# Two row maxima of a wide tile joined into one, in a NaN-ignoring row maximum

## The chip, the cores and the metric

The kernel runs on one core of one Trainium2 chip. The core has engines that work side by side, each with its own instruction stream: VectorE (DVE in the profile), ScalarE (ACT), GpSimd (POOL), TensorE (PE, unused here) and SyncE (SP), which issues the DMA transfers. They wait for one another through semaphores. The 16 DMA engines move data between the device's main memory (HBM) and the on-chip memory, which has 128 partitions.

The metric is the time of one execution on the device, in microseconds (us). Lower is better.

## The reference

```python
batch, seq, dim = 32, 2048, 2048
x = np.random.randn(batch, seq, dim).astype(np.float32)
mask = np.random.rand(batch, seq, dim) < 0.1
x[mask] = np.nan
...
return np.nanmax(x, axis=-1).astype(np.float32)
```

The input has 65,536 rows of 2048 float32 numbers, 512 MiB, a tenth of them NaN. The output is the maximum of each row without the NaNs, 256 KiB. Every input byte is read once, and little is done with it.

## The kernel before

**Tiles and quarter rows.** Each partition gets 512 rows, and a quarter row (Q = 512 elements, 2 KiB in a partition) is the unit of all tables. `TILES` is a list of tiles; each says how it is loaded, how it is worked on, and how the maxima are taken. Tile 0 has 4 quarter rows. Tiles 1 to 32 are the wide ones: 32 quarter rows, that is 8 whole rows in each of 128 partitions, 8 MiB, loaded by one DMA. Tiles 33 to 68 are cut in other ways and mostly have 28 quarter rows.

**What is done to a tile.** Ahead of the maximum the upper 16 bits of every element are turned into a key and then written back, in place, such that a NaN becomes something small. The steps for a wide tile are:

- *Key* on ScalarE (ACT, the program's line 299): three passes over 12, 12 and 8 quarter rows, as each is free. They read the upper halves of `xt` (an access of every second 16-bit number) and write them back as unsigned keys. A pass waits only for the load of its tile.
- *Write* on GpSimd (POOL, L309): one multiply-add that turns keys into the number's upper half again. Of the first 12 quarter rows, 5 are written by VectorE (a TENSOR_SCALAR over 128x2560, which the profile shows under L316, the line of the helper) and 7 by POOL (128x3584). Then POOL writes 12 (128x6144) and 8 (128x4096). A write waits for its key pass.
- *Maximum* on VectorE (L316, TENSOR_REDUCE into `acc`): the last list of a tile says over how many quarter rows each step goes. `128x3` in a profile row is a step over 3 rows, that is 12 quarter rows; `128x2` is 8, `128x5` is 20. A step waits for the writes of the quarter rows it covers.

In one tile's entry `([12], [(5, -1), 7])` reads: a key pass of 12, then a write of 5 on VectorE (-1) and one of 7 on POOL.

**What sets the order.** Nothing reorders instructions: each engine runs its own in the order in which the loop over tiles writes them. For each key pass the loop issues the pass, then the writes whose keys are then complete, then the maxima (`maxima`) whose quarter rows have all been given a write. VectorE's stream in a wide tile is thus: its write of 5, and the maxima. The class `Order` adds the semaphore waits, leaving out those that another wait already covers.

**Buffers and loads.** There are three buffers (`BUFS = 3`), used in turn. The load of tile n goes into the buffer of tile n - 3 and waits for the last maximum of that tile:

```python
                if state["red"] == len(reds):
                    free[number % BUFS] = [state["end"]]
```

All loads are issued from SP's queue, one behind the other, by line 495 (the first one by L286). The results are stored at the end (L591), after some steps (L331, L345 on POOL, L323 on VectorE) that turn rows of nothing but NaN into NaN, one part of the rows at a time. POOL's steps for a part stand two to four tiles after the part's last tile (two for the wide ones).

Of the kernel before, what the change touches and what calls it, by code (L numbers as in the profile page):

```python
# [15 lines left out]

TILES = (
    [([4], [([4], [4])], [4])]
    + [([32], [([12], [(5, -1), 7]), ([12], [12]), ([8], [8])], [12, 12, 8])] * 32
# [622 lines left out]
```

## Time and profile before

| | us |
|---|---|
| median of 3 runs | 1252.22 (1252.11 to 1252.24) |
| the profiled execution | 1252.06 |
| its span in the profile | 1250.3 |
| VectorE busy | 1164.8 |
| ScalarE busy | 1151.3 |
| GpSimd busy | 1060.2 |

The span is the time between the first and the last recorded event; the execution's own time is 1.8 us longer. A row of the chain of waits or of the timeline begins with its start and its length in us, then the engine, the line, and what was written from what; "x2" means that two instructions stand in one row, and the brackets tell how long the engine was idle ahead of it and for whom. A row of the groups has, behind the bar, the busy time in us, the mean of one instruction in ns, and the idle time ahead of such instructions. In the list of DMA issues the last number is the median time from issue to landing in us.

### The profile page before, as it was taken

How to read it: one execution, taken by the hardware profiler on the slowest of the kernel's cores; microseconds unless marked ns; L12 is line 12 of the kernel's file. 1: busy time of each engine (PE TensorE's matmuls, PEld its weight loads, DVE VectorE, ACT ScalarE, POOL GpSimd, SP SyncE). 2: the span in 40 equal slices, each digit the busy share in tenths (PEclk: the TensorE clock that was granted, in tenths of full speed). 3: DMA queues.
4: the chain of work that ended last, by engine and by line, in shares of the span. 5: the costliest groups of instructions: out<-in, count | busy, mean ns of one | idle time of the engine just before them, and what ended most of it. 6: DMA issues, size and time to landing. Idle time of an engine off the chain costs nothing.

```text
span 1250.3 us, 1057 instructions
## 1 busy us (share of the span) xinstructions
DVE 1164.8 (93%) x252; ACT 1151.3 (92%) x294; POOL 1060.2 (85%) x253
## 2 busy tenths in 40 slices
DVE  0799999999999999999999998988889989999999
ACT  3999999999999999999999999898888789999998
POOL 0888788887988888888899998977999887999988
DMA  9999999999999999999999999999999999999997
GB/s 411 428 436 436 436 436 436 436 437 434 436 436 432 432 432 428 434 430 434 434 431 438 433 439 440 433 427 431 440 428 440 426 439 431 431 430 428 432 427 309
DMA packets 17240, 537.21 MB, mean 430 GB/s; under 512 B 2640, under 2 KB 2640, under 8 KB 5712
## 3 DMA queue, kind: packets, MB, share of 16 engines
q1 hardware_dynamic: 17232, 537.14, 99.5%
q14 instruction: 8, 0.07, 0.0%
HBM read 536.87 MB, written 0.26 MB: 430 GB/s over the span
## 4 chain that ended last, share of the span: by engine, by line
DMA 38%; DVE 25%; ACT 23%; POOL 14%; issue 1%; SPq 0%; ACTq 0%
DMA xt<-in_x_dram 38%; DVE acc L316 24%; ACT xt L299 21%; POOL xt L309 14%; ACT kt L299 2%; SPq L495 0%; SPq L286 0%; DVE acc L323 0%; SPq L637 0%; ACTq L183 0%; SPq L293 0%
## 5 line engine op out<-in xcount | busy, mean ns | idle before, releaser
L316 DVE TENSOR_REDUCE acc<-xt 128x3 f32<-128x6144 f32 (+3 forms) x219 | 1114.6, 5135 | 64.2 <-POOL xt L309 56.7
L309 POOL TENSOR_SCALAR xt<-xt 128x3584 int16<-128x3584 uint16 (+9 forms) x204 | 926.3, 4541 | 162.8 <-ACT xt L299 152.9
L299 ACT ACTIVATE xt<-xt 128x6144 uint16<-128x6144 int16 (+12 forms) x236 | 1006.3, 4361 | 62.8 <-DMA xt<-in_x_dram 61.9
L309 POOL TENSOR_SCALAR xt<-kt 128x4096 int16<-128x4096 uint16 (+10 forms) x34 | 128.8, 3789 | 21.2 <-ACT kt L299 19.7
L299 ACT ACTIVATE kt<-xt 128x4096 uint16<-128x4096 int16 (+10 forms) x42 | 118.9, 2852 | 29.7 <-DMA xt<-in_x_dram 29.4
L316 DVE TENSOR_SCALAR xt<-xt 128x2560 int16<-128x2560 uint16 x32 | 52.6, 1644 | 19.0 <-ACT xt L299 19.0
L299 ACT ACTIVATE xt<-kt 128x1536 int16<-128x1536 uint16 (+6 forms) x14 | 29.6, 2112 | 0.2
L331 POOL TENSOR_SCALAR late<-acc 128x112 int32<-128x112 f32 (+1 forms) x5 | 2.8, 558 | 0.4
L299 ACT ACT_TABLE_LOAD x1 | 1.3, 1283 | 1.3 <-SPq L293 1.3
L345 POOL TENSOR_TENSOR acc<-acc,late 128x112 int32<-128x112 int32 (+1 forms) x5 | 2.0, 397 | 0.4
L351 POOL MEMSET scalars<- 128x1 f32 x1 | 0.1, 98 | 0.9 <-SPq L293 0.9
L623 POOL MEMSET const-float32-0.0<- 128x1 f32 x1 | 0.1, 98 | 0.2 <-issue 0.2
L299 ACT ACTIVATE scalars<-scalars 128x1 f32<-128x1 f32 x1 | 0.2, 203 | 0.0
L323 DVE SCALAR_TENSOR_TENSOR acc<-acc 128x7 f32<-128x7 f32 x1 | 0.2, 166 | 0.0
L623 POOL MEMSET const-bfloat16-1.0<- 128x1 bf16 x1 | 0.1, 101 | 0.0
L623 POOL MEMSET const-uint8-127<- 128x1 uint8 x1 | 0.1, 101 | 0.0
L623 POOL MEMSET const-float32-1.0<- 128x1 f32 x1 | 0.1, 98 | 0.0
## 6 DMA issues: line engine op xcount, KB each, us to landing
xt<-in_x_dram SPq DMA_DIRECT2D x20, 7168.0 KB, 23.3
xt<-in_x_dram SPq DMA_DIRECT2D x5, 2304.0 KB, 25.6
xt<-in_x_dram SPq DMA_DIRECT2D x2, 5632.0 KB, 19.6
xt<-in_x_dram SPq DMA_DIRECT2D x3, 3584.0 KB, 25.0
xt<-in_x_dram SPq DMA_DIRECT2D x2, 4352.0 KB, 17.3
xt<-in_x_dram SPq DMA_DIRECT2D x2, 4096.0 KB, 19.7
xt<-in_x_dram SPq DMA_DIRECT2D x1, 7680.0 KB, 24.2
xt<-in_x_dram SPq DMA_DIRECT2D x9, 768.0 KB, 25.3
```

What stands on the lines that cost most here:

```text
L299: lambda: nc.scalar.activation(**kw),
L309: lambda: nc.gpsimd.tensor_scalar(**kw),
L316: return order.add("dve", nc.vector, lambda: do(**kw), deps)
L323: lambda: engine.scalar_tensor_tensor(out=acc, in0=acc, scalar=0.0, in1=acc, op0=ALU.mult, op1=ALU.add),
L331: lambda: engine.tensor_scalar(out=none, in0=acc, scalar1=LEAST, scalar2=float(0x00400000), op0=ALU.is_lt, op1=ALU.mult,),
L345: lambda: engine.tensor_tensor(out=bits, in0=bits, in1=none, op=ALU.add),
L351: e_top = order.add("pool", nc.gpsimd, lambda: nc.gpsimd.memset(top, EDGE), [])
L623: nc = _bacc.Bacc("TRN2", target_bir_lowering=False, num_devices=1)
```

## The change

One number list in the table changes, for the 32 wide tiles. The maxima go over 12 and 20 quarter rows, where they went over 12, 12 and 8:

```diff
 TILES = (
     [([4], [([4], [4])], [4])]
-    + [([32], [([12], [(5, -1), 7]), ([12], [12]), ([8], [8])], [12, 12, 8])] * 32
+    + [([32], [([12], [(5, -1), 7]), ([12], [12]), ([8], [8])], [12, 20])] * 32
```

Each wide tile has one VectorE instruction less, 32 in all. Keys, writes and loads are the same, as are the streams of ScalarE, POOL and SP. What stands on VectorE at the start of the program, in the tiles 0, 1 and 2, is this before (a row gives line, operation, what is written from what, its shape, and in brackets the engine whose semaphore it waits for):

```order
L316 TENSOR_REDUCE acc<-xt 128x1 [waits order_pool]
L316 TENSOR_SCALAR xt<-xt 128x2560 [waits order_act]
L316 TENSOR_REDUCE acc<-xt 128x3 [waits order_dve,order_pool]
L316 TENSOR_REDUCE acc<-xt 128x3 [waits order_pool]
L316 TENSOR_REDUCE acc<-xt 128x2 [waits order_pool]
L316 TENSOR_SCALAR xt<-xt 128x2560 [waits order_act]
L316 TENSOR_REDUCE acc<-xt 128x3 [waits order_dve,order_pool]
```

And this is the same place now:

```order
L316 TENSOR_REDUCE acc<-xt 128x1 [waits order_pool]
L316 TENSOR_SCALAR xt<-xt 128x2560 [waits order_act]
L316 TENSOR_REDUCE acc<-xt 128x3 [waits order_dve,order_pool]
L316 TENSOR_REDUCE acc<-xt 128x5 [waits order_pool]
L316 TENSOR_SCALAR xt<-xt 128x2560 [waits order_act]
L316 TENSOR_REDUCE acc<-xt 128x3 [waits order_dve,order_pool]
```

The step over 3 rows that waited for POOL's write of 12 quarter rows and the step over 2 rows that waited for its write of 8 have become a step over 5 rows that waits for the later of the two; the next tile's TENSOR_SCALAR stands behind it.

At the end of the wide tiles VectorE goes from tile 32 to tile 33, which has no write on VectorE and keeps its maxima of 12, 12 and 8. In the difference of the two streams, this is the place:

```order
 L316 TENSOR_SCALAR xt<-xt 128x2560 [waits order_act]
 L316 TENSOR_REDUCE acc<-xt 128x3 [waits order_dve,order_pool]
-L316 TENSOR_REDUCE acc<-xt 128x3 [waits order_pool]
-L316 TENSOR_REDUCE acc<-xt 128x2 [waits order_pool]
+L316 TENSOR_REDUCE acc<-xt 128x5 [waits order_pool]
 L316 TENSOR_REDUCE acc<-xt 128x3 [waits order_pool] x2
 L316 TENSOR_REDUCE acc<-xt 128x2 [waits order_act,order_pool]
```

Behind tile 32's step over 5 rows follow tile 33's steps over 3, 3 and 2 rows, which are as before.

## The prediction

> **What bounds the kernel now.** I read the page first: busy shares, the DMA row of the slices, and the queue.
>
> ```profile
> span 1250.3 us, 1057 instructions
> DVE 1164.8 (93%) x252; ACT 1151.3 (92%) x294; POOL 1060.2 (85%) x253
> DMA  9999999999999999999999999999999999999997
> GB/s 411 428 436 436 436 436 436 436 437 434 436 436 432 432 432 428 434 430 434 434 431 438 433 439 440 433 427 431 440 428 440 426 439 431 431 430 428 432 427 309
> q1 hardware_dynamic: 17232, 537.14, 99.5%
> ```
>
> Three compute engines are over 85% busy, but the DMA engines are busy all the time. The kernel ends when its bytes are in, so a compute engine can lengthen it only by leaving the DMA queue empty. A change that speeds up compute has almost nothing to win; one that delays the release of a buffer can lose. So the next view is what the queue that issues the loads (SP) waits for, and then the chain of waits, for one ring of three tiles (tile 14 landing at 276.81, its buffer going to tile 17).
>
> ```profile
> SPq L495 <- DVE acc L316: 1150.5, 66, 43.5
> ```
> ```profile
> 276.81 0.02 issue
> 276.83 13.93 ACT xt L299 x2
> 290.76 0.07 issue
> 290.84 7.01 POOL xt L309
> 297.85 0.02 issue
> 297.87 10.89 DVE acc L316 x2
> 308.76 0.02 issue
> 308.78 25.91 DMA xt<-in_x_dram
> 334.69 0.02 issue
> ```
>
> SP waits for VectorE alone: for a tile's last maximum. From landing to the next load's issue go two key passes on ACT, the 12 quarter row write of POOL, and two maxima on DVE: 276.81 to 308.78, 31.97 us. The ring is 334.69 - 276.81 = 57.88 us, 19.3 for each tile. The 25.91 us of the load contain a time in which it stands behind the load before it. The timeline shows how long:
>
> ```profile
> 303.24 4.16 POOL L309 TENSOR_SCALAR xt<-xt 128x3584 int16<-128x3584 uint16 x1 [0.58 <-ACT xt L299]
> 308.67 1.60 DVE L316 TENSOR_SCALAR xt<-xt 128x2560 int16<-128x2560 uint16 x1
> 310.09 11.81 POOL L309 TENSOR_SCALAR xt<-xt 128x6144 int16<-128x6144 uint16 x2 [2.69 <-ACT xt L299]
> 310.37 6.55 DVE L316 TENSOR_REDUCE acc<-xt 128x3 f32<-128x6144 f32 x1
> 315.42 18.51 ACT L299 ACTIVATE xt<-xt 128x6144 uint16<-128x6144 int16 x3 [0.84 <-DMA xt<-in_x_dram]
> 317.13 10.88 DVE L316 TENSOR_REDUCE acc<-xt 128x3 f32<-128x6144 f32 x2 [0.21 <-POOL xt L309]
> ```
>
> The load before lands at 315.4 (ACT starts at 315.42 after waiting for it), 6.6 us after the issue at 308.78. So 6.6 us is the whole cover of the release. It has to hold a new delay and the time h that a load needs beside its transfer, from issue to first byte and from last byte to semaphore. Bounds for h:
>
> ```profile
> 0.74 0.37 SPq L286 DMA_DIRECT2D xt<-in_x_dram  x1
> 5.62 2.47 ACT L299 ACTIVATE xt<-xt 128x2048 uint16<-128x2048 int16 x1 [2.78 <-DMA xt<-in_x_dram]
> ```
> ```profile
> out_dram<-acc SPq DMA_DIRECT2D x1, 224.0 KB, 2.3
> ```
>
> The first load (4 quarter rows, 1.05 MB; 2.4 us at the 436 GB/s of the early slices) takes 4.88 us on an empty queue: h = 2.5. The store of 224 KB takes 2.3 us, 0.5 of it transfer: h = 1.8. I take 2.15, the middle: the first is the same kind of load but the program's first, the second runs warm but goes the other way. The Trainium skill, page "DMA: Bandwidth & Descriptors", section "Anatomy of one DMA", gives about 2.0 us of fixed cost (fitted on another issue path); with that figure an estimate of the sum below would be 38 us in place of 40. Both rows agree within 0.5 us.
>
> **The change, part by part.** Durations by shape, from the groups kept apart:
>
> ```profile
> L316 DVE TENSOR_REDUCE acc<-xt 128x3 f32<-128x6144 f32 x96 | 628.7, 6552 | 33.8 <-POOL xt L309 30.5
> L316 DVE TENSOR_REDUCE acc<-xt 128x2 f32<-128x4096 f32 x67 | 294.4, 4410 | 2.6 <-POOL xt L309 2.6
> L309 POOL TENSOR_SCALAR xt<-xt 128x4096 int16<-128x4096 uint16 x40 | 189.6, 4740 | 3.2 <-ACT xt L299 0.2
> L316 DVE TENSOR_SCALAR xt<-xt 128x2560 int16<-128x2560 uint16 x32 | 52.6, 1644 | 19.0 <-ACT xt L299 19.0
> L316 DVE TENSOR_REDUCE acc<-xt 128x5 f32<-128x10240 f32 x1 | 10.8, 10820 | 2.3 <-POOL xt L309 2.3
> ```
>
> Removed: one VectorE instruction in each of 32 tiles. The two maxima take 10.89 us back to back, one of 20 quarter rows 10.82: 0.07 x 32 = 2.2 us of VectorE. I count nothing for it: the 99.5% of the queue covers it.
>
> Moved, first step: the 20 quarter row maximum waits for POOL's last write (8 quarter rows), where the 12 row maximum waited only for the write before. From landing: 13.93 + 0.07 (ACT, start), 7.01 (POOL, 12), 0.08 and 4.74 (POOL, 8), 0.04, 10.82 and 0.03 = 36.7 us. The release is 36.7 - 32.0 = 4.75 us later. That alone would lie within 6.6 - 2.15 = 4.5 us of cover, but for 0.3.
>
> Moved, second step: behind that maximum on VectorE stands the next tile's write of 5 quarter rows (TENSOR_SCALAR, 128x2560), and behind it that tile's first maximum. In the row of before it runs at 308.67, in the hole POOL has while it waits for ACT (303.24 + 4.16 = 307.40 to 310.09). Started 4.75 us later, at 313.4, it falls into POOL's 12 row write (310.09 to 317.10). What these two do to each other:
>
> ```profile
> 31.93 1.64 DVE L316 TENSOR_SCALAR xt<-xt 128x2560 int16<-128x2560 uint16 x1 [18.98 <-ACT xt L299]
> 31.98 5.57 POOL L309 TENSOR_SCALAR xt<-xt 128x3584 int16<-128x3584 uint16 x1 [21.34 <-ACT xt L299]
> ```
> ```profile
> 637.64 1.66 DVE L316 TENSOR_SCALAR xt<-xt 128x2560 int16<-128x2560 uint16 x1
> ```
> ```profile
> 638.41 7.77 POOL L309 TENSOR_SCALAR xt<-xt 128x6144 int16<-128x6144 uint16 x1 [2.54 <-ACT xt L299]
> ```
>
> At 31.98 POOL starts 0.05 us behind VectorE's write, and its 7 quarter rows take 5.57 us, not 4.16: 1.41 more, nearly all of the 1.59 they overlap. At 638.41 the overlap is 0.89, and the 12 rows take 7.77 against 7.01. So the two exclude one another, while maxima run beside POOL's writes without stretching either. In every such row VectorE was first. The trace has none where POOL is. The bounds: VectorE's write waits for nothing (0), or for the rest of POOL's write, 3.7 us at the first collision. I take the second, since the nearest rows show the later one waiting for the whole of the earlier.
>
> The Trainium skill says the same of the case not seen: page "SBUF — State Buffer", section "Who interferes with whom", calls the SBUF port pair that the two share an exclusive lock, whoever issues first keeps it for the whole instruction, and a reduce takes no part in it. The trace agrees for VectorE first (1.41 us); by the rule the sum would be the one below, by "no wait" the first rival's.
>
> With the wait, from landing: 14.0 + 7.01 to the end of POOL's 12 row write; then 1.65 for VectorE's write, 0.05, 6.55 for the first maximum, 10.82 less 0.08 of overlap, 0.03: 40.05 us. POOL's 8 row write, held for 1.65, ends at 14.0 + 7.01 + 1.65 + 4.8 = 27.5, ahead of the 20 row maximum (29.2), so it costs nothing. The state keeps itself up: VectorE's cycle is 1.65 + 0.05 + 6.55 + 10.75 = 19.0 against 19.3 between landings, so the next write comes 0.3 us before POOL's 12 row write ends, and is held again. The release is 40.05 - 32.0 = 8.05 us later; of this 6.6 - 2.15 = 4.45 is covered, and the queue stands dry for 3.6 us in each ring of three tiles.
>
> Rings: tile 1 has the order of 31.93 (VectorE first), so the first held write is tile 2's, and its load is tile 5's. Loads 5, 8, ... 35 make 11 rounds: 11 x 3.6 = 40 us.
>
> Behind the wide tiles the code is unchanged, but VectorE arrives late:
>
> ```profile
> 658.22 6.55 DVE L316 TENSOR_REDUCE acc<-xt 128x3 f32<-128x6144 f32 x1 [1.12 <-POOL xt L309]
> ```
>
> Tile 33's first maximum started at 658.22 after 1.12 us of idling; now VectorE is free some 6 us later than that. Tiles 33 to 35 have no VectorE write, so the lag falls by idle time of about a us a tile. I add 2 us, between 0 and 4. Nothing else moves: ACT waits for landings alone, SP has only later loads behind the waiting one, and POOL's final steps (L331) wait for a VectorE step of two tiles back.
>
> Sum: the profiled span 1250.3 + 40 + 2 = 1292.3; the profiled execution took 1252.06, 1.8 over its span, and stands 0.2 below the median of 1252.22. Forecast 1294 us. With h from 1.8 to 2.5 and 0 to 4 behind: 11 x 3.25 = 36 to 11 x 3.95 = 43, so 1288 to 1299.
>
> **Rivals.** *VectorE's write is not held* (ends on the other side: not slower). Place: the collision at 313.4. For it: no row shows VectorE waiting for POOL. Against it: the 1.41 us of the reverse. The release is then 4.75 late, and h decides: under 1.85 the cover holds and nothing is lost, 1252; at 2.15 it is 0.3 x 11 = 3; at 2.5, 0.65 x 11 = 7, 1259.
>
> *VectorE cuts in*: it takes its 1.65 us at once and POOL's write is stretched. Then 36.7 + 1.65 = 38.4, 6.4 late, 1.95 dry a ring: 11 x 1.95 = 21, 1273 (1270 to 1279). For it: POOL gave way in all rows; against: there it came second.
>
> *VectorE is held through both of POOL's writes*, which follow each other within 0.08 us. Then its write starts at 14.0 + 7.01 + 0.08 + 4.74 = 25.8, the release at 44.9, 12.9 late, 8.45 dry a ring: 93 us and some 5 behind, 1350. Against it: the start of a POOL write needs nothing exclusive (the row at 310.09, overlapped by 0.18, has 11.81 for both writes, no more than 7.01 + 0.08 + 4.74), so a waiting write finds a gap between the two.
>
> *VectorE's saved instruction is felt*: at most 2.2 us faster, against a queue 99.5% busy.
>
> **How the numbers follow.** Held once 0.52; not held 0.20; cuts in 0.12; held twice 0.12; anything else, a gain included, 0.04. A measurement of this kernel can tell about 0.2%, 2.5 us. Faster 0.01; the same 0.12, the lower half of "not held" and a little more; slower 0.87. The range from 1252 to 1300 takes in the first three cases; 1350 stays outside with its 0.12. The likeliest case alone has 1288 to 1299.
>
> **What would show it.** Right: the 128x5 group has 33 instructions of 10.82; every third landing comes about 3.6 us late, so the ring is 61.5 us, not 57.9; the slices up to 640 us fall from 436 to some 410 GB/s; VectorE's 128x2560 row grows (0.3 to 4 us of waiting in its 1644 ns) or stands behind an idle time that no semaphore ends; POOL's 128x4096 row in wide tiles grows by up to 1.6 us. Wrong: a 128x2560 row still at 1.64 us in the middle of POOL's write (not held, or cutting in if POOL's 128x6144 row is 8.6), or one near 6 to 12 us (held twice). h would be wrong if the gap between one landing and the next, in a load issued late, is off 19.3 by other than the issue's delay.

## The result, and the profile after

The changed kernel takes 1294.5 us (median of 4 runs, 1293.4 to 1297.6) against 1252.2 before: a ratio of 1.034, with an interval of 1.033 to 1.036. It is slower by 42 us. The forecast was 1294, slower. The profiled execution is the longest of the four, 1297.6 us, so its own numbers add up to 45 us and not to 42.

The page of the changed kernel:

```profile
span 1295.8 us, 1025 instructions
DVE 1217.2 (94%) x220; ACT 1153.3 (89%) x294; POOL 1093.2 (84%) x253
GB/s 421 419 390 405 405 421 397 413 421 389 419 390 417 392 397 411 411 368 421 388 433 378 447 425 439 439 425 434 443 427 429 446 420 438 432 428 433 429 427 319
q1 hardware_dynamic: 17232, 537.14, 97.5%
```

In the first half of the span, the wide tiles, the DMA engines now move some 405 GB/s, not 433; in the second half nothing has changed. VectorE is busy for 52 us longer with 32 instructions less, and POOL for 33 us longer with the same instructions. The groups by shape say where:

```profile
L316 DVE TENSOR_REDUCE acc<-xt 128x5 f32<-128x10240 f32 x33 | 356.7, 10810 | 8.9 <-POOL xt L309 8.9
L309 POOL TENSOR_SCALAR xt<-xt 128x6144 int16<-128x6144 uint16 x40 | 281.2, 7031 | 79.8 <-ACT xt L299 79.4
L309 POOL TENSOR_SCALAR xt<-xt 128x4096 int16<-128x4096 uint16 x40 | 229.2, 5731 | 3.4 <-ACT xt L299 0.3
L316 DVE TENSOR_SCALAR xt<-xt 128x2560 int16<-128x2560 uint16 x32 | 110.2, 3445 | 19.0 <-ACT xt L299 19.0
```

The joined maximum costs what it should, 10.81 us. VectorE's write has gone from 1644 ns to 3445, POOL's write of 8 quarter rows from 4740 to 5731. The timeline of the first collision shows the two together:

```profile
58.08 7.05 POOL L309 TENSOR_SCALAR xt<-xt 128x6144 int16<-128x6144 uint16 x1 [2.68 <-ACT xt L299]
61.31 5.26 DVE L316 TENSOR_SCALAR xt<-xt 128x2560 int16<-128x2560 uint16 x1
61.42 0.33 SPq L495 DMA_DIRECT2D xt<-in_x_dram  x1
63.43 7.00 ACT L299 ACTIVATE xt<-xt 128x6144 uint16<-128x6144 int16 x1 [0.79 <-DMA xt<-in_x_dram]
```

VectorE's write starts 3.2 us into POOL's, at 61.31, and ends at 66.57, 1.44 us after POOL's has ended at 65.13. Its own work is 1.6 us, so it stood still until POOL was all but done. POOL's row is not stretched (7.05). The load of tile 4 is issued 2.0 us ahead of the landing before it (63.41), where it was 6.8.

The chain of waits no longer runs through the DMA queue in the wide tiles, but nearly all along VectorE: its write, then two maxima, again and again. The view counts the time in which the write is held as VectorE's work and does not say what it waits for, so it does not show that VectorE is the bound; the run with loads in two parts, below, tells.

```profile
103.33 4.54 DVE xt L316
...
107.96 17.28 DVE acc L316 x2
125.24 3.72 DVE xt L316
...
129.05 6.55 DVE acc L316
```

### The profile page after: what moved, and what is told of

It is laid out like the page before. It is cut to its first block, busy times and chain, and to the rows that moved or that the text cites. A ratio compares the mean times of both kernels' runs of the same rounds, so it can differ in the third digit from the quotient of the medians.

```text
span 1295.8 us, 1025 instructions
## 1 busy us (share of the span) xinstructions
DVE 1217.2 (94%) x220; ACT 1153.3 (89%) x294; POOL 1093.2 (84%) x253
## 3 DMA queue, kind: packets, MB, share of 16 engines
q1 hardware_dynamic: 17232, 537.14, 97.5%
## 4 chain that ended last, share of the span: by engine, by line
DVE 61%; DMA 19%; POOL 10%; ACT 8%; issue 1%; SPq 0%; DVEq 0%; ACTq 0%
DVE acc L316 53%; DMA xt<-in_x_dram 19%; POOL xt L309 10%; DVE xt L316 8%; ACT xt L299 6%; ACT kt L299 2%; SPq L495 0%; DVEq L183 0%; SPq L286 0%; DVE acc L323 0%; SPq L637 0%; ACTq L183 0%; SPq L293 0%
## 5 line engine op out<-in xcount | busy, mean ns | idle before, releaser
L316 DVE TENSOR_REDUCE acc<-xt 128x3 f32<-128x6144 f32 (+4 forms) x187 | 1109.3, 5987 | 57.4 <-POOL xt L309 50.8
L309 POOL TENSOR_SCALAR xt<-xt 128x3584 int16<-128x3584 uint16 (+9 forms) x204 | 959.2, 4702 | 175.2 <-ACT xt L299 164.9
L309 POOL TENSOR_SCALAR xt<-kt 128x4096 int16<-128x4096 uint16 (+10 forms) x34 | 128.8, 3790 | 21.5 <-ACT kt L299 19.8
L316 DVE TENSOR_SCALAR xt<-xt 128x2560 int16<-128x2560 uint16 x32 | 110.2, 3445 | 19.0 <-ACT xt L299 19.0
```

What stands on the lines that cost most here:

```text
L309: lambda: nc.gpsimd.tensor_scalar(**kw),
L316: return order.add("dve", nc.vector, lambda: do(**kw), deps)
```

## The experiments

All but the two with a small instruction change the entry of the wide tiles; edits are against the changed kernel where nothing else is said; "..." stands for `[([32], [`. "Release" is the time from the landing of a tile to the issue of the load that takes its buffer; "landing time" is from that issue to the landing (medians over the loads of tiles 5 to 32, from the trace). Before, they are 32.1 and 25.9 us; after, 40.0 and 22.1.

**No write on VectorE, maxima as changed.** POOL writes all of the first 12 quarter rows, so there is nothing to be held.

```diff
-    + ...([12], [(5, -1), 7]), ([12], [12]), ([8], [8])], [12, 20])] * 32
+    + ...([12], [12]), ([12], [12]), ([8], [8])], [12, 20])] * 32
```

> Maxima of 12 and 20 as in the changed kernel, but POOL writes all of the first 12 quarter rows and VectorE has no write in the wide tiles, so nothing can be held. Theory (held write, 3.3 us of the 3.9 us that a ring lost): the release comes at 36.8 us from landing, 4.85 late, 0.7 over the cover with h = 2.45, so 11 x 0.7 = 8 us over before: 1260, ratio 1.006. Rival (the late release alone costs it, with a larger h): stays near 1294.

Measured: 1284.5 us, ratio 1.025 (1.023 to 1.027). Neither expectation held. The release is where it was expected, 36.95 us. One ring in the chain of waits of this kernel:

```profile
203.77 24.34 DMA xt<-in_x_dram
228.11 0.02 issue
228.13 7.01 ACT xt L299
235.14 0.07 issue
235.21 7.09 POOL xt L309
242.31 0.08 issue
242.38 6.99 POOL xt L309
249.38 0.08 issue
249.45 4.73 POOL xt L309
254.18 0.02 issue
254.21 10.83 DVE acc L316
265.04 0.02 issue
265.05 24.60 DMA xt<-in_x_dram
```

From one issue to the next the ring is 61.3 us, against 57.9 before. Compute is 36.9 of it, as worked out, but the load takes 24.3 to 24.6 us, where 19.3 of transfer and h = 2.45 would be 21.75. So h, taken as one number, is wrong here.

**The control without a VectorE write,** maxima of 12, 12 and 8:

> The control: maxima of 12, 12 and 8, POOL writes everything, no VectorE write in the wide tiles. POOL has 7.0 + 7.0 + 4.7 = 18.8 us a tile against 19.3 between landings. Both theories: 1252. If POOL alone became the bound, this would be slower, and the other run without a write could not be read.

Measured: 1251.9 us, ratio 1.000 (0.999 to 1.001). POOL is not the bound, and the other runs without a write can be read. VectorE has 32 instructions less here than in the kernel before (its 32 writes), and nothing is won.

**Maxima of 12, 4 and 16, with and without the VectorE write.** The release alone would be 2.6 us late.

```diff
-    + ...([12], [(5, -1), 7]), ([12], [12]), ([8], [8])], [12, 20])] * 32
+    + ...([12], [(5, -1), 7]), ([12], [12]), ([8], [8])], [12, 4, 16])] * 32
```

> VectorE's write stays; maxima of 12, 4 and 16 quarter rows. By release alone the tile would end at 25.85 + 8.7 = 34.6 us, 2.6 late, inside the cover of 4.2. Theory (held write): VectorE's next write then comes at 34.6 - 19.3 = 15.3 us from its tile's landing, after POOL's write of 12 has started at 14.0, is held to 21.0, and the state keeps itself up as in the changed kernel: about 1294. Rival (late release alone): 1252.

> Maxima of 12, 4 and 16 with no VectorE write. Release at 34.7 us, 2.7 late, inside the cover of 4.2. Both theories: 1252; with the run that keeps the write it says what the write costs at the same order of maxima (theory: 42 us; rival: nothing).

Measured: 1294.4 us with the write (1.034, 1.032 to 1.035), 1260.3 without (1.007, 1.005 to 1.008). The first is the held write's number to the microsecond; its first held write, at the same place as above:

```profile
59.35 7.31 DVE L316 TENSOR_SCALAR xt<-xt 128x2560 int16<-128x2560 uint16 x1
```

The second misses the expected 1252 by 8 us: a release only 2.8 us late, issued on average 4.4 us ahead of the landing before it, already costs something. At this order of maxima the write's being held is worth 34 us, at 12 and 20 only 10.

**Later still, with nothing held.** Maxima of 8 and 24, and of 4 and 28, without a VectorE write:

```diff
-    + ...([12], [12]), ([12], [12]), ([8], [8])], [12, 20])] * 32
+    + ...([12], [12]), ([12], [12]), ([8], [8])], [8, 24])] * 32
```

> No VectorE write in the wide tiles, maxima of 8 and 24: release at 39.0 us from landing with nothing that could be held, nearly where the held write puts it in the changed kernel (40.05). Theory A (a load that is issued when every DMA lane has run dry lands in 21.9 us, one that is issued while some lanes still work lands in 24.5, since the lane that gets its share last carries its lag on): the ring is 39.0 + 21.9 = 60.9, 3.0 over before, 11 x 3.0 = 33 and some 3 behind: 1288. Theory B (a late load always lands in 24.5): 11 x 5.6 = 62, 1316. Either way a run near the changed kernel's 1294 says that the hold acts through the release time alone.

> As above with maxima of 4 and 28: release at 41.1 us. Theory A: ring 41.1 + 21.9 = 63.0, 11 x 5.1 = 56 and some 4 behind: 1312. Theory B: 11 x 7.7 = 85 and more: 1340.

Measured: 1287.5 us (1.029, 1.027 to 1.030) and 1309.4 us (1.046, 1.044 to 1.047). Theory A's 1288 and 1312, not theory B's 1316 and 1340. From 12 and 20 to 8 and 24 the release comes 2.1 us later in each ring and the whole costs only 3 us more, since the load lands faster. In one row each, the median from issue to landing of the 32 loads of 8 MiB, for maxima of 12 and 20, of 8 and 24, and for the changed kernel:

```profile
xt<-in_x_dram SPq DMA_DIRECT2D x32, 24.3
```
```profile
xt<-in_x_dram SPq DMA_DIRECT2D x32, 22.0
```
```profile
xt<-in_x_dram SPq DMA_DIRECT2D x32, 22.3
```

What differs is seen in the trace's DMA events. A load is spread over 16 DMA engines, and each raises the load's semaphore once when its part is in. First and last of the 16, for the load of tile 13 (us):

```
kernel                       issue   landed before    first part in  last part in  issue to last
before                       231.03  236.97-237.63    256.28         257.56        26.5
changed                      248.98  248.82-249.23    270.23         270.76        21.8
no write, maxima 12 and 20   245.29  244.68-247.41    266.78         269.99        24.7
no write, maxima 8 and 24    246.49  245.89-246.68    267.62         268.15        21.7
```

In the second and fourth row the load before had ended on every engine by 0.25 us after the issue, and the engines finish within 0.5 us of each other. In the third, some were done 0.6 us before the issue and some worked on for 2.1 us; they finish within 3.2 us, and the tile waits for the last one. Such a distance between the first and the last engine, once there, stays for several loads (2.7, 3.2, 3.3, 3.5 us for tiles 12 to 15 with maxima of 12 and 20, 4.2 for tile 18, then 0.9 for tile 19).

The state at the issue alone does not decide, so theory A's condition does not hold as it was put. With maxima of 4 and 28 the loads of tiles 5, 6, 8, 9, 11 and 12 were issued 2.1 to 2.5 us ahead of the landing before, with all 16 engines still at work, and landed in 21.7 to 22.0 us; the load before had ended on all engines within 0.4 to 0.7 us. In the changed kernel the loads of tiles 9 and 12, issued 2.5 and 2.6 us ahead, landed as fast (21.8 and 21.9). The five loads of 23 us and more with maxima of 8 and 24 or of 4 and 28 were issued 1.6 to 1.9 us ahead, but others issued so took 22. What the two runs support is thus that 22 us hold where the engines end together, and more where they have come apart.

How they come apart stays open. In the first late load with maxima of 12 and 20 and no write, issued at 61.79, the parts start between 63.1 and 64.6, and the first packets take 2.6 to 3.4 us, where later ones take 2.42. But first packets of 2.5 to 3.3 us stand in the changed kernel's load of tile 13 as well, and its engines stay together.

**One small instruction.** In the kernel before, VectorE does the same operation once more, over 64 elements into a scratch tile, right behind each of its writes; in the other run a maximum over the same 64 elements.

```diff
                 if back == "dve":
                     e = dve([e], nc.vector.tensor_scalar, **kw)
+                    dve(
+                        [e],
+                        nc.vector.tensor_scalar,
+                        out=junk.bitcast(i16)[:, 1::2],
+                        in0=room(number)[:, a : a + 64].bitcast(u16)[:, 1::2],
...
```

> The kernel before with one more VectorE instruction behind each VectorE write: the same operation over 64 elements into a scratch tile. It comes some 0.2 us after POOL's write of 12 has begun. Theory (the write excludes POOL's writes, the later waits for the earlier's end): it is held for about 6.7 us, every tile ends that much later, the next VectorE write is then held too: far slower, 1320 to 1350. Rival (held only because of its length, or not at all): 0.1 us a tile, 1252 to 1256.

> The same place, a maximum over 64 elements in place of the write. Theory: maxima never wait for POOL: 0.15 us a tile of VectorE, 19.1 of 19.3, so 1252 to 1254. If this is as slow as the other, an instruction at this place costs by itself and not through POOL.

Measured: 1340.8 us (1.071, 1.069 to 1.073) and 1251.9 us (1.000, 0.999 to 1.001). The small write at tile 2, and the group of the small maxima in the other run:

```profile
58.35 11.89 POOL L310 TENSOR_SCALAR xt<-xt 128x6144 int16<-128x6144 uint16 x2 [2.68 <-ACT xt L300]
58.43 7.05 DVE L317 TENSOR_SCALAR junk<-xt 128x64 int16<-128x64 uint16 x1
```
```profile
L317 DVE TENSOR_REDUCE junk<-xt 128x1 f32<-128x64 f32 x32 | 7.0, 220 | 1.1
```

Starting 0.08 us behind POOL's write, 64 elements take 7.05 us, the whole of POOL's write; a maximum at the same place takes 0.22. So the order of arrival decides, and the length of VectorE's instruction does not. This is the case that the trace of before did not have. The rule of the Trainium skill's page "SBUF — State Buffer", section "Who interferes with whom", that whoever issues first keeps the shared port pair for its whole instruction, agrees with this row. At the later tiles it is mostly the long write that comes late and is held, at 25 of the 32 behind POOL's write of 8, and the release comes at 44.8 us (median); the small write behind it takes 0.2 us at 25 tiles.

**Maxima of 12, 8 and 12,** with the VectorE write: nearly the order of before, the release alone 0.5 us late.

```diff
-    + ...([12], [(5, -1), 7]), ([12], [12]), ([8], [8])], [12, 20])] * 32
+    + ...([12], [(5, -1), 7]), ([12], [12]), ([8], [8])], [12, 8, 12])] * 32
```

> VectorE's write stays; maxima of 12, 8 and 12. The release alone is 0.5 us late, far inside the cover. But the last maximum now starts at the end of POOL's last write, and VectorE's write delays POOL by their overlap, so the overlap should grow by some 0.6 us a tile until, after two or three tiles, POOL starts first and the write is held. Theory: from then on as in the changed kernel, 1290 to 1295. Rival (a write is held only behind a maximum as long as 16 or 20): 1252.

Measured: 1290.4 us (1.031, 1.029 to 1.033). VectorE's writes of tiles 2 to 5, with the maxima between them left out:

```profile
57.08 1.66 DVE L316 TENSOR_SCALAR xt<-xt 128x2560 int16<-128x2560 uint16 x1
...
76.96 1.69 DVE L316 TENSOR_SCALAR xt<-xt 128x2560 int16<-128x2560 uint16 x1
...
96.92 1.57 DVE L316 TENSOR_SCALAR xt<-xt 128x2560 int16<-128x2560 uint16 x1
...
116.69 8.09 DVE L316 TENSOR_SCALAR xt<-xt 128x2560 int16<-128x2560 uint16 x1
```

POOL's write of 12 starts at 58.15, 77.54, 96.90 and 116.24. VectorE is ahead by 1.07 and 0.58 us, then level (0.02 us behind, but it is POOL's write that grows, to 8.5 us), and at tile 5 behind by 0.45: the write is held for 6.5 us and the tiles stay in that state.

**The changed kernel with loads in two parts.** The first 12 quarter rows of a buffer are loaded anew when the first maximum of its old tile is done, the other 20 after the last. ACT still waits for both.

```diff
-    + [([32], [([12], [(5, -1), 7]), ([12], [12]), ([8], [8])], [12, 20])] * 32
+    + [([12, 20], [([12], [(5, -1), 7]), ([12], [12]), ([8], [8])], [12, 20])] * 32
...
-                    before + lanes[turn],
+                    (
+                        [next(e for d, e in steps[number - BUFS] if d >= at + c)]
+                        if BUFS < number <= 32
+                        else before
+                    )
+                    + lanes[turn],
...
```

The lines left out keep each maximum's event in `steps`, and let ACT's passes wait for both parts.

> The changed kernel with each wide load cut into 12 and 20 quarter rows; the first part goes out after the first maximum of the buffer's old tile, the second after the last. ACT still starts a tile when both parts are in. Theory (the held write and the late maximum cost only by letting the DMA queue run dry): VectorE's write is held as before, 2 to 5 us each, but the first part is issued at about 29.3 us from landing, 9 us ahead of the end of the load before, and the second 5.8 us ahead of the end of the first: the queue stays full and the time is 1252. Rival (VectorE or POOL has become the bound of the wide tiles): stays near 1294.

Measured: 1256.9 us, ratio 1.004 (1.002 to 1.005). In the wide tiles the queue is full again, though VectorE's writes are still held. A window over them (start and end, length, busy time and instructions of VectorE, ScalarE and GpSimd, clock, DMA share, GB/s) and the group of the writes:

```profile
40.00:600.00 560.00, 550.47 (x86) 535.01 (x87) 497.87 (x91) 1.00 1.00 433
```
```profile
L316 DVE TENSOR_SCALAR xt<-xt 128x2560 int16<-128x2560 uint16 x32 | 69.1, 2158 | 19.1 <-ACT xt L299 19.1
```

The queue moves 433 GB/s at a DMA share of 1.00. VectorE, busy or held for 550 of the 560 us, keeps pace, so it is not the bound. The writes take 2158 ns in place of 1644: held by some 0.5 us each, where 2 to 5 were expected and the changed kernel has 1.8. With the loads in time the hold stays short. Tile 32 lands at 625.4 us, 1 us later than before. The other 3.6 us are lost at the handover to the narrow tiles, whose loads still wait for a whole wide tile: tile 35's last part lands 4.6 us later than before.

**The same loads on the kernel before,** with ACT starting when the first 12 quarter rows are in (loads cut and issued as in the run before, maxima of 12, 12 and 8, ACT's waits unchanged):

> The kernel before with loads of 12 and 20 quarter rows, each issued when the old tile's maxima over its place are done, and ACT starting when the first 12 are in. The wide tiles were bound by the DMA queue at 99.5%, so theory: no gain there, 1252, at best 1 to 2 us less where the wide tiles hand over to the narrow ones. Slower if smaller transfers move fewer bytes a second.

Measured: 1253.2 us, ratio 1.001 (1.000 to 1.002). Loads issued 21 to 25 us ahead of the landing before win nothing where the queue was never empty. No run was measurably faster than the kernel before.

## Why the prediction was right, and where it was not

- *What bounds the kernel*: right. The share of the queue fell from 99.5% to 97.5%, and with the queue filled again (loads in two parts) the loss was gone but for 5 us. The removed instruction was worth nothing.
- *The late maximum*: right in its size; without a write the release went from 32.2 to 36.95 us, 4.75 forecast.
- *The held write*: right. VectorE's write waits for POOL's to end and POOL's next write then waits for it (5731 ns, 4740 before). The release was forecast at 40.05 us and is 40.0. The gap between two writes of POOL is enough for VectorE, so the "held twice" rival did not occur in the changed kernel.
- *The state keeps itself up*: right, and shown best by the maxima of 12, 8 and 12, where it takes hold after three tiles.
- *The cover and h*: this step failed. "6.6 - 2.15 = 4.45 is covered, and the queue stands dry for 3.6 us in each ring" took h as one number between 1.8 and 2.5. Where the 16 engines end a load together, a late load lands in 21.7 to 22.0 us, so h is 2.4 to 2.7, the upper row and a little more; with maxima of 12 and 20 and no write, where they end mostly 2 to 4 us apart, it takes 24.3, h = 5. The changed kernel has both kinds (22.3 in the mean), and its ring in the profiled execution is 62.2 us where 61.5 was forecast. The loss also starts a tile earlier than forecast: the load of tile 4, behind tile 1's joined maximum and with no write held yet, lands 2.3 us late. Up to tile 32, ten of the eleven rounds and so 36 us by the forecast, 42 us were lost by the landings (666.5 against 624.4).
- *The rival "not held"*: its price, 1252 to 1259, was wrong for the same reason. It was tried: 1284. So the forecast came out near for a reason only half understood. Of the 42 us, the late release would have cost 32 alone; the held write adds 3.0 us to the release, and 1.9 of them come back in the landing time (22.3 in the mean against 24.2), for the engines are closer together (1.0 us apart at the end of a load in the mean, against 2.8).
- *Every third landing late by 3.6 us*: in kind only. Two of three come late, by 2.2 and 1.7 us (median gaps of 21.5, 21.0 and 19.4).
- *Behind the wide tiles*: 2 us forecast, between 0 and 4; nothing measured. The eleventh round ends with tile 35's load, 45.7 us late, and the last load of all is 45.5 late.
- *The number*: that 1294 met the median within a microsecond is luck. In the profiled execution the eleven rounds cost 45.7 us and not 40, nothing came behind them, and the median execution is 3 us shorter than the profiled one.

## What to carry to other kernels

Before joining two steps, look at when the joined step ends, not at what it costs: here it ended 4.75 us later, and its end was what the next load waited for. Ask then what stands behind it on its engine, and whether that instruction excludes another engine's; its new place can turn a neighbour that ran in a hole into one that waits. A cover just above the fixed cost of one transfer may not be enough: of 6.6 us of cover here, a release 2.8 us later left 3.8, more than the 2.5 that a load needs beside its transfer when the engines are together, and still cost 8 us; one 4.75 us later left 1.85 and cost 32, where 0.65 us missing in each of eleven rounds would make 7.

## What the runs showed of the hardware

- A VectorE write of 64 elements that arrives 0.08 us behind a GpSimd write waits for all of it (7.05 us, against 0.2 when free). A waiting VectorE write is let in between two GpSimd writes that follow each other within 0.08 us: the second then waits for it (5.93 us in place of 4.74).
- The 16 DMA engines can come apart when loads are issued late. With maxima of 12 and 20 and no VectorE write they finish a load up to 4.2 us apart, and an 8 MiB load takes 24.3 us from issue to landing (median). With maxima of 8 and 24, and of 4 and 28, they mostly end within 1.1 us of each other and a load takes 22.0 and 21.9, also where it was issued 2.1 to 2.5 us ahead of the landing before.
- The kernel before stood near the edge itself. Its VectorE write overlapped POOL's by 0.18 us at 310 us into the run and by 0.89 at 638, where 1.65 would have put POOL first.
